# The experts' gate and up biases as three bf16 parts over 96 of 128 rows, in one pass, in place of fp32 and fp32r products over 64 rows

## The chip, the cores and the metric

The kernel runs on one core of a Trainium2 chip. The metric is the device time of one execution in microseconds (us), median of the runs shown. The engines are TensorE (PE), VectorE (DVE), ScalarE (ACT), GpSimd (POOL) and SyncE (SP), the last of which issues most DMA transfers.

## The reference, cut to what matters

Two blocks follow each other on 512 tokens of width 1024. The first (a Mamba-2 and forgetting-attention mixer and a feed-forward layer) is only touched at its end. The second has a sliding-window attention with a gated MLP, a layer norm, and 32 routed experts, of which each token takes four. All is fp32:

```python
def expert_block(args):
    xb, e = args
    gt = jnp.minimum(xb @ w_gate[e] + b_gate[e], SWIGLU_LIMIT)
    up = jnp.clip(xb @ w_up[e] + b_up[e], -SWIGLU_LIMIT, SWIGLU_LIMIT)
    hid = gt * jax.nn.sigmoid(SWIGLU_ALPHA * gt) * (up + 1.0)
    return hid @ w_down[e] + b_down[e]
```

The change concerns the two terms `b_gate[e]` and `b_up[e]`, rows of two matrices of 32 x 1024. They are added in fp32 precision.

## The kernel before, in words

Block 1 fills the first 853 us or so, the attention and gated MLP of block 2 run until about 1060 us, the router follows, and the experts run from about 1075 to 2210 us. Each instruction stands in the queue of its engine in an order that a scheduler works out from the program; the order is fixed when the kernel is built.

Matrices of weights come in fp32 from HBM. In most places one fp32 product is made of three products in fp32r, a form that goes through the array in one pass: weight and operand are split into a rounded high part (`wh`, `eh`, ...) by an ACT copy and a low part (`wl`, `el`, ...) by a DVE subtraction, and PE adds high x high, low x high and high x low into the same accumulator.

The experts are taken in the order of a rank, the fullest first for all but the first four. Even ones from the fifth on (14 of them) are small: they have 64 token rows. The other 18 are large, with 128 rows; the one at place 17 (`PS`) has two blocks of rows. Per expert there are matrices for gate (G), up (U) and down (D), each in four loads of 1 MB (`eraw`, L1061, issued on SP) into a ring of 14 slots. The order of the loads is gate and up of expert e, then down of expert e - 1.

A large expert goes through `expert_mm`: ACT casts `eh` (L1316), DVE subtracts `el` (L1317), and PE runs three fp32r products (L1382 to L1384) for each of 8 k and each half of 512 columns. A small expert goes through `expert_mm64`: PE multiplies the fp32 rows as loaded (L1398), with 64 columns of the array for one half of the outputs and the other 64 columns for the other half, so that both halves run side by side. Then DVE clamps (L1472 and L1478 are the clamps of gate and up for small experts), ACT takes the silu, and transposes (`pt_`, L1416 for the large ones) make the operands of the next products.

The bias enters as the first product of each accumulation. `bgu` holds `b_gate` in rows 0 to 63 and `b_up` in rows 64 to 127: in each, 32 rows of the rounded high part and 32 rows of the rest. The other operand picks the expert: `selP` has, in column e, a one in the row of the expert that stands at place e, repeated for each 32 rows; a column of it is broadcast over the output rows. `selr` is the same for the first four, whose place is their number. For a large expert this is a product of 64 rows in fp32r for each half (L1372); for a small one it is a product of 64 rows and 64 columns in fp32 for each half (L1391).

`bgu` is made once, at L819 to L832, when the feed-forward layer of block 1 ends: four small loads (L829) into `b0`, a tile of the ring `wraw` of three slots that also carries `w_fo`, the last matrix of block 1, and `w_in`, the first of block 2. An ACT copy makes the high part (L830), two DVE subtractions the low one (L832). Around it lies the end of the feed-forward layer: for each of 8 tiles ACT and DVE add the residual (L763, L764), subtract (L199) and sum (L206, and L207 partly on POOL), and PE makes the column sums of the norm from the last sums (L166, tile `pns`, and L171). Then the projections of block 2 start (L117 with `x2H`).

`ranks` (L1276) makes `selP` when the counts of the experts are known; `places` uses it as fp32 too. `seB` is the selection for extra blocks that are only run when an expert has more tokens than its rows hold.

Of the kernel before, what the change touches and what calls it, by code (L numbers as in the profile page):

```python
# [10 lines left out]
F32 = mybir.dt.float32  # L11
F32R = mybir.dt.float32r
# [9 lines left out]
P = 128  # L22
# [28 lines left out]
def tile_kernel(ctx, tc, I, out, dbg=None):  # L51
# [764 lines left out]
        dve.memset(tv[:, c, :, 1], float(c * P))  # L816
    dve.memset(tv[:, :, :, 2], 1.0)

    selr = pr2.tile([P, E], F32R, name="selr")  # L819
    ident4 = ident.rearrange("p (a e) -> p a e", a=4)  # L820
    selt = sb.tile([P, 2, E], F32, name="selt")
    dve.tensor_add(selt, ident4[:, :2], ident4[:, 2:])
    dve.tensor_add(selr, selt[:, 0], selt[:, 1])
    b0 = wring.tile([P, D], F32, name="b0", tag="wraw", bufs=3)
    bgu = const.tile([P, D], F32R, name="bgu", tag="csil")
    for i, nm in enumerate(("b_gate", "b_up")):
        for q in range(2):
            r = slice(64 * i + 32 * q, 64 * i + 32 * q + E)
            sp.dma_start(b0[r], I[nm])  # L829
    act.copy(bgu, b0)  # L830
    for r in (slice(32, 64), slice(96, 128)):
        dve.tensor_sub(bgu[r], b0[r], bgu[r].bitcast(F32))  # L832
    lnv = sb.tile([P, 2, 512], F32, name="lnv")
    sp.dma_start(lnv.rearrange("p a b -> p (a b)")[:, None, :], I["lnv"].partition_broadcast(P))
    wsp = sb.tile([P, 8, P], F32, name="wsp")
# [409 lines left out]
        slot_gate(ps[:, :, 3:6], n, gsl[:, sl])  # L1245

    posP = sb.tile([P, 4, E], F32, name="posP", tag="posP")
    selP = sb.tile([P, E], F32R, name="selP")
    permi = sb.tile([P, E], I32, name="permi")
    permf = sb.tile([P, 2, E], F32, name="permf")  # L1250
    rks = sb.tile([P, E], F32, name="rks")
# [24 lines left out]
    def ranks():  # L1276

        w = sm.tile([P, 4, E], F32, name="xw", tag="gt")
        key, t, kc = w[:, 0], w[:, 1], w[:, 2]
        dve.scalar_tensor_tensor(key, cnt, 64.0, iota_e, op0=OP.mult, op1=OP.subtract)  # L1280
        dve.tensor_scalar(key[:, :PRE], iota_e[:, :PRE], -1.0, 1e6, op0=OP.mult, op1=OP.add)
        for i, src in enumerate((key, cnt)):
            dve.scalar_tensor_tensor(t, src, 1.0, selr.bitcast(F32), op0=OP.mult, op1=OP.mult, accum_out=kc[:, i:i + 1])
        dve.tensor_copy(cntc, kc[:, 1:2])
        dve.tensor_scalar(t, key, kc[:, 0:1], None, op0=OP.is_gt)
        dve.tensor_reduce(kc[:, 2:3], t, axis=AX.X, op=OP.add)
        dve.tensor_scalar(selP, rks, kc[:, 2:3], None, op0=OP.is_equal)
        ps = pg.tile([2 * E, T], F32, name="ppgT", tag="pt", bufs=1)
        box["posgT"] = posgT = sm.tile([2 * E, T], F32, name="posgT", tag="up")
        for c in range(4):  # L1290
            pe.transpose(ps[:, c * P:(c + 1) * P], posg[:, c].rearrange("p a e -> p (a e)"), ident)
        act.copy(posgT, ps)

    def places():

        sf, posgT = selP.bitcast(F32), box["posgT"]
        ps = pg.tile([P, 2, 16, E], F32, name="pposP", tag="pt", bufs=1)
        for i, src in enumerate((rowe, cntc)):
            pe.matmul(ps[:, 0, 4 + i], src[:E].to_broadcast([E, P]), sf[:E], start=True, stop=True)
        for c in range(4):  # L1300
            for i in range(2):
                r = slice(i * E, (i + 1) * E)
                pe.matmul(ps[:, i, c], posgT[r, c * P:(c + 1) * P], sf[r], start=True, stop=True)
        dve.tensor_copy(permf, ps[:, 0, 4:6])
        dve.tensor_copy(permi, permf[:, 0])
        dve.tensor_copy(posP, ps[:, 0, :4])
        split_gates(PRE, E, ps[:, 1, :4])
# [58 lines left out]
    def expert_mm(xs, pss, bias=None, sel_=None, mid=None, get=ring_k):  # L1366

        if bias is not None:
            r = slice(64 * bias, 64 * bias + 64)
            for ps in pss:  # L1370
                for hf in range(2):
                    pe.matmul(ps[:, hf], sel_[r].to_broadcast([64, P]), bgu[r, hf * 512:(hf + 1) * 512],  # L1372
                              start=True, stop=False)
        for k in range(8):
            for go in (mid or {}).get(k, ()):
                go()
            for raw in get(k):
                h, l = split_k(raw)
            for (xh, xl), ps in zip(xs, pss):
                for hf in range(2):  # L1380
                    s_ = slice(hf * 512, (hf + 1) * 512)
                    pe.matmul(ps[:, hf], xh[:, k], h[:, s_], start=k == 0 and bias is None, stop=False)  # L1382
                    pe.matmul(ps[:, hf], xl[:, k], h[:, s_], start=False, stop=False)  # L1383
                    pe.matmul(ps[:, hf], xh[:, k], l[:, s_], start=False, stop=k == 7)  # L1384

    def expert_mm64(x, ps, bias=None, sel_=None, mid=None):

        for hf in range(2):
            if bias is not None:
                r = slice(64 * bias, 64 * bias + 64)  # L1390
                pe.matmul(ps[hf * 64:(hf + 1) * 64, 0], sel_[r].bitcast(F32).to_broadcast([64, 64]),  # L1391
                          bgu[r, hf * 512:(hf + 1) * 512].bitcast(F32), start=True, stop=False)
        for k in range(8):
            for go in (mid or {}).get(k, ()):
                go()
# [172 lines left out]

    ixB = sb.tile([P, 2], I32, name="ixB")
    gcB = sb.tile([P, 1], F32, name="gcB")  # L1570
    seB = sb.tile([P, 1], F32R, name="seB")

    def block(er, cl):

# [79 lines left out]
    for e in range(E):  # L1654
# [14 lines left out]
            mid[1] = [next_h(u_, "A", e - 1)]  # L1669
        if e == PS + 1:  # L1670
            mid[3] = [two_h]
        sel_ = (selr if e < PRE else selP)[:, e:e + 1]
        if small[e]:
            expert_mm64(x[0], pG[0], 0, sel_, mid)
        else:
# [213 lines left out]
```

## Time and profile before

| what | value |
|---|---|
| time, median of 3 runs | 2257.95 us (2257.52 to 2262.35) |
| the profiled execution | 2258.27 us, of which the span of the profile is 2256.5 us |
| mean granted TensorE clock | 0.973 of full speed |
| PE, DVE, ACT, POOL busy | 94%, 64%, 49%, 8% of the span |
| data moved | 554.53 MB, 246 GB/s over the span |

A group line of the profile has the source line, the engine, the operation, output <- inputs, the size of the tile of the array or of the instruction, a count and times. A matrix product in fp32 leaves two records, one in fp32r one. The products overlap in the pipeline of the array, so the time from one start to the next (the step) tells more than the duration of one record. The engines do not count waiting as busy.

### The profile page before, as it was taken

The page shows a single profiled execution, that of the slowest core. Times are in us where ns is not written, and L with a number is a line of the kernel's source. Part 1 is how long each engine was busy: PE and PEld are TensorE (multiplying, and loading weights), DVE is VectorE, ACT ScalarE, POOL GpSimd, SP SyncE. Part 2 cuts the span into 40 slices and gives each one's busy share as a digit, 9 for nine tenths or more (in the row PEclk, how much of TensorE's full clock was granted, in tenths as well). Part 3 has the DMA queues.
Part 4 walks back from the last instruction along what each step waited for, and adds up shares of the span by engine and source line. Part 5 has one row for each costly group of instructions (what it writes and reads, how often), then busy time and mean ns, then how long its engine had stood idle before and what let it go on. Part 6 is the DMA issues. An engine that isn't in the chain of part 4 may idle for free. (4 is left out here: it accounts for less than half of the span.)

```text
span 2256.5 us, 27626 instructions
## 1 busy us (share of the span) xinstructions
PE 2118.9 (94%) x9746; PEld 1495.8 (66%) x9747; DVE 1448.4 (64%) x2620; ACT 1104.4 (49%) x1511; POOL 190.4 (8%) x167
## 2 busy tenths in 40 slices
PE   7999999989999998999899999999999999899995
PEld 5787776677878886777676665445565665445653
DVE  7999978885224647655798566456553465645665
ACT  2576666434344434763576455334542455334553
POOL 0001100110000001003101110001000101001001
PEclk9999999989999998998899999999999999999998
DMA  8454414225332223136899999999997999999892
GB/s 284 139 169 145 132 61 134 94 87 174 96 100 86 94 96 97 55 123 229 291 336 347 392 401 394 405 397 349 396 358 273 367 401 396 391 365 384 337 375 81
DMA packets 153488, 554.53 MB, mean 246 GB/s; under 512 B 13440, under 2 KB 13824, under 8 KB 153344
## 3 DMA queue, kind: packets, MB, share of 16 engines
q1 hardware_dynamic: 143888, 527.54, 63.0%
q0 software_dynamic: 9456, 25.18, 4.5%
q8 instruction: 78, 1.28, 0.2%
q14 instruction: 66, 0.54, 0.1%
HBM read 537.91 MB, written 19.99 MB: 247 GB/s over the span
## 5 line engine op out<-in xcount | busy, mean ns | idle before, releaser
L1317 DVE TENSOR_TENSOR el<-eraw,eh 128x1024 fp32r<-128x1024 f32 x428 | 502.3, 1219 | 92.8 <-ACT eh L1316 81.5
L1316 ACT CAST eh<-eraw 128x1024 fp32r<-128x1024 f32 x432 | 439.5, 1048 | 137.3 <-PE ps_G L1383 49.1
L113 DVE TENSOR_TENSOR wl<-wraw,wh 128x1024 fp32r<-128x1024 f32 (+1 forms) x150 | 180.3, 1202 | 209.0 <-ACT wh L112 208.4
L112 ACT CAST wh<-wraw 128x1024 fp32r<-128x1024 f32 (+1 forms) x150 | 154.0, 1026 | 265.1 <-PE pff L118 89.8
L1384 PE MATMUL ps_G<-el,BH 128*128 128x512 f32 x288 | 114.8, 399 | 1.7 <-DVE el L1317 1.5
L1382 PE MATMUL ps_D<-eh,AH 128*128 128x512 f32 x272 | 110.7, 407 | 6.0 <-ACT eh L1316 6.0
L1382 PE MATMUL ps_G<-eh,BH 128*128 128x512 f32 x288 | 115.2, 400 | 0.0
L1384 PE MATMUL ps_D<-el,AH 128*128 128x512 f32 x272 | 111.5, 410 | 3.3 <-DVE el L1317 3.2
L1383 PE MATMUL ps_G<-eh,BL 128*128 128x512 f32 x288 | 113.3, 393 | 0.0
L1383 PE MATMUL ps_D<-eh,AL 128*128 128x512 f32 x272 | 108.9, 400 | 0.0
L1398 PE MATMUL ps_D<-eraw,AW 128*64 128x512 f32 x448 | 106.5, 603 | 0.0
L1398 PE MATMUL ps_G<-eraw,BW 128*64 128x512 f32 x448 | 103.8, 598 | 0.0
L117 PE MATMUL pff<-h2H,wh 128*128 128x512 f32 x256 | 100.7, 397 | 2.0 <-ACT h2H L733 2.0
L1384 PE MATMUL ps_U<-el,BH 128*128 128x512 f32 x256 | 102.1, 399 | 0.3 <-DVE el L1317 0.3
L117 PE MATMUL pfo<-fh,wh 128*128 128x512 f32 x256 | 100.3, 394 | 1.9 <-ACT fh L757 1.9
L118 PE MATMUL pff<-h2L,wh 128*128 128x512 f32 x256 | 101.5, 396 | 0.0
L119 PE MATMUL pff<-h2H,wl 128*128 128x512 f32 x256 | 100.3, 392 | 1.1 <-DVE wl L113 1.1
L118 PE MATMUL pfo<-fl,wh 128*128 128x512 f32 x256 | 101.4, 397 | 0.0
L1398 PE MATMUL ps_U<-eraw,BW 128*64 128x512 f32 x448 | 101.1, 604 | 0.0
L1382 PE MATMUL ps_U<-eh,BH 128*128 128x512 f32 x256 | 100.6, 393 | 0.0
L1383 PE MATMUL ps_U<-eh,BL 128*128 128x512 f32 x256 | 100.4, 392 | 0.0
L119 PE MATMUL pfo<-fh,wl 128*128 128x512 f32 x256 | 100.2, 394 | 0.0
(956 smaller groups left out, 4502.7 us busy)
## 6 DMA issues: line engine op xcount, KB each, us to landing
eraw<-in_w_gate_dram SPq DMA_DIRECT2D x128, 1024.0 KB, 10.8
eraw<-in_w_up_dram SPq DMA_DIRECT2D x127, 1024.0 KB, 11.0
eraw<-in_w_down_dram SPq DMA_DIRECT2D x127, 1024.0 KB, 10.8
wada<-in_w_ada_dram SPq DMA_DIRECT2D x48, 512.0 KB, 4.0
wraw<-in_w_fo_dram SPq DMA_DIRECT2D x32, 512.0 KB, 3.4
wraw<-in_w_ff_in_dram SPq DMA_DIRECT2D x26, 512.0 KB, 3.5
wraw<-in_w_out_dram SPq DMA_DIRECT2D x16, 512.0 KB, 3.8
wraw<-in_w_xs_dram SPq DMA_DIRECT2D x8, 512.0 KB, 6.3
```

What stands on the lines that cost most here:

```text
L112: act.copy(h, w)
L113: dve.tensor_sub(l, w, h.bitcast(F32))
L117: pe.matmul(ps, wh, xh, start=first, stop=False)
L118: pe.matmul(ps, wh, xl, start=False, stop=False)
L119: pe.matmul(ps, wl, xh, start=False, stop=last)
L1316: act.copy(h, raw_k)
L1317: (pool if ns[0] < 4 else dve).tensor_sub(l, raw_k, h.bitcast(F32))
L1382: pe.matmul(ps[:, hf], xh[:, k], h[:, s_], start=k == 0 and bias is None, stop=False)
L1383: pe.matmul(ps[:, hf], xl[:, k], h[:, s_], start=False, stop=False)
L1384: pe.matmul(ps[:, hf], xh[:, k], l[:, s_], start=False, stop=k == 7)
L1398: pe.matmul(ps[hf * 64:(hf + 1) * 64, 0], x[:, k], raw[:, hf * 512:(hf + 1) * 512], start=k == 0 and bias is None, stop=k == 7)
```

## The change

Each bias becomes three bf16 parts: the rounded value, the rounded rest and the rounded rest of that, 32 rows each, so 96 rows; rows 96 to 127 are filled with zeros by POOL. `bgu` is [128, 2, 1024] in bf16, with gate and up side by side in the columns. The selection gets bf16 copies (`selq`, `selPq`) over all 128 rows. The product of a bias is then one bf16 product over 128 rows for each half, for large (now L1382) and small experts (now L1400) alike. The set-up makes the parts on ACT (copies) and DVE (subtractions), for each bias in a `b0` tile of its own, with three loads each.

```diff
--- before.py
+++ after.py
@@ -816,20 +816,29 @@
         dve.memset(tv[:, c, :, 1], float(c * P))
     dve.memset(tv[:, :, :, 2], 1.0)
 
-    selr = pr2.tile([P, E], F32R, name="selr")
+    selr = pr2.tile([P, E], F32, name="selr")
     ident4 = ident.rearrange("p (a e) -> p a e", a=4)
     selt = sb.tile([P, 2, E], F32, name="selt")
     dve.tensor_add(selt, ident4[:, :2], ident4[:, 2:])
     dve.tensor_add(selr, selt[:, 0], selt[:, 1])
-    b0 = wring.tile([P, D], F32, name="b0", tag="wraw", bufs=3)
-    bgu = const.tile([P, D], F32R, name="bgu", tag="csil")
+    selq = pr2.tile([P, E], BF16, name="selq")
+    dve.tensor_copy(selq, selr)
+    bgu = const.tile([P, 2, D], BF16, name="bgu", tag="csil")
+    pool.memset(bgu[3 * E:], 0.0)
     for i, nm in enumerate(("b_gate", "b_up")):
-        for q in range(2):
-            r = slice(64 * i + 32 * q, 64 * i + 32 * q + E)
-            sp.dma_start(b0[r], I[nm])
-    act.copy(bgu, b0)
-    for r in (slice(32, 64), slice(96, 128)):
-        dve.tensor_sub(bgu[r], b0[r], bgu[r].bitcast(F32))
+        b0 = wring.tile([P, D], F32, name="b0", tag="wraw", bufs=3)
+        for q in range(3):
+            sp.dma_start(b0[q * E:(q + 1) * E], I[nm])
+        for q in range(3):
+            r = slice(q * E, 3 * E)
+            if q == 1:
+                for r in (slice(E, 2 * E), slice(2 * E, 3 * E)):
+                    dve.tensor_sub(b0[r], b0[r], bgu[r, i])
+                    act.copy(bgu[r, i], b0[r])
+            else:
+                if q == 2:
+                    dve.tensor_sub(b0[r], b0[r], bgu[r, i])
+                act.copy(bgu[r, i], b0[r])
     lnv = sb.tile([P, 2, 512], F32, name="lnv")
     sp.dma_start(lnv.rearrange("p a b -> p (a b)")[:, None, :], I["lnv"].partition_broadcast(P))
     wsp = sb.tile([P, 8, P], F32, name="wsp")
@@ -1245,7 +1254,8 @@
         slot_gate(ps[:, :, 3:6], n, gsl[:, sl])
 
     posP = sb.tile([P, 4, E], F32, name="posP", tag="posP")
-    selP = sb.tile([P, E], F32R, name="selP")
+    selP = sb.tile([P, E], F32, name="selP")
+    selPq = sb.tile([P, E], BF16, name="selPq")
     permi = sb.tile([P, E], I32, name="permi")
     permf = sb.tile([P, 2, E], F32, name="permf")
     rks = sb.tile([P, E], F32, name="rks")
@@ -1280,11 +1290,12 @@
         dve.scalar_tensor_tensor(key, cnt, 64.0, iota_e, op0=OP.mult, op1=OP.subtract)
         dve.tensor_scalar(key[:, :PRE], iota_e[:, :PRE], -1.0, 1e6, op0=OP.mult, op1=OP.add)
         for i, src in enumerate((key, cnt)):
-            dve.scalar_tensor_tensor(t, src, 1.0, selr.bitcast(F32), op0=OP.mult, op1=OP.mult, accum_out=kc[:, i:i + 1])
+            dve.scalar_tensor_tensor(t, src, 1.0, selr, op0=OP.mult, op1=OP.mult, accum_out=kc[:, i:i + 1])
         dve.tensor_copy(cntc, kc[:, 1:2])
         dve.tensor_scalar(t, key, kc[:, 0:1], None, op0=OP.is_gt)
         dve.tensor_reduce(kc[:, 2:3], t, axis=AX.X, op=OP.add)
-        dve.tensor_scalar(selP, rks, kc[:, 2:3], None, op0=OP.is_equal)
+        dve.tensor_scalar(selPq, rks, kc[:, 2:3], None, op0=OP.is_equal)
+        dve.tensor_copy(selP, selPq)
         ps = pg.tile([2 * E, T], F32, name="ppgT", tag="pt", bufs=1)
         box["posgT"] = posgT = sm.tile([2 * E, T], F32, name="posgT", tag="up")
         for c in range(4):
@@ -1293,7 +1304,7 @@
 
     def places():
 
-        sf, posgT = selP.bitcast(F32), box["posgT"]
+        sf, posgT = selP, box["posgT"]
         ps = pg.tile([P, 2, 16, E], F32, name="pposP", tag="pt", bufs=1)
         for i, src in enumerate((rowe, cntc)):
             pe.matmul(ps[:, 0, 4 + i], src[:E].to_broadcast([E, P]), sf[:E], start=True, stop=True)
@@ -1366,10 +1377,9 @@
     def expert_mm(xs, pss, bias=None, sel_=None, mid=None, get=ring_k):
 
         if bias is not None:
-            r = slice(64 * bias, 64 * bias + 64)
             for ps in pss:
                 for hf in range(2):
-                    pe.matmul(ps[:, hf], sel_[r].to_broadcast([64, P]), bgu[r, hf * 512:(hf + 1) * 512],
+                    pe.matmul(ps[:, hf], sel_.to_broadcast([P, P]), bgu[:, bias, hf * 512:(hf + 1) * 512],
                               start=True, stop=False)
         for k in range(8):
             for go in (mid or {}).get(k, ()):
@@ -1387,9 +1397,8 @@
 
         for hf in range(2):
             if bias is not None:
-                r = slice(64 * bias, 64 * bias + 64)
-                pe.matmul(ps[hf * 64:(hf + 1) * 64, 0], sel_[r].bitcast(F32).to_broadcast([64, 64]),
-                          bgu[r, hf * 512:(hf + 1) * 512].bitcast(F32), start=True, stop=False)
+                pe.matmul(ps[hf * 64:(hf + 1) * 64, 0], sel_.to_broadcast([P, 64]),
+                          bgu[:, bias, hf * 512:(hf + 1) * 512], start=True, stop=False)
         for k in range(8):
             for go in (mid or {}).get(k, ()):
                 go()
@@ -1568,7 +1577,7 @@
 
     ixB = sb.tile([P, 2], I32, name="ixB")
     gcB = sb.tile([P, 1], F32, name="gcB")
-    seB = sb.tile([P, 1], F32R, name="seB")
+    seB = sb.tile([P, 1], BF16, name="seB")
 
     def block(er, cl):
 
@@ -1669,7 +1678,7 @@
             mid[1] = [next_h(u_, "A", e - 1)]
         if e == PS + 1:
             mid[3] = [two_h]
-        sel_ = (selr if e < PRE else selP)[:, e:e + 1]
+        sel_ = (selq if e < PRE else selPq)[:, e:e + 1]
         if small[e]:
             expert_mm64(x[0], pG[0], 0, sel_, mid)
         else:
```

The scheduler orders the rest anew. On PE, at the down products of one small expert (`ps_D`, L1398 before, L1407 now), the two halves of the up bias of the next small expert (L1391 before, L1400 now) stand as follows; `pt_` are transposes. Before:

```order
L1398 MATMUL ps_D<-eraw,AW 64x512 x4
L1391 MATMUL ps_U<-bgu,selP 64x512
L1398 MATMUL ps_D<-eraw,AW 64x512 x4
L1416 MATMUL pt__15412<-ident,up 128x128 x5
L1398 MATMUL ps_D<-eraw,AW 64x512 x4
L1416 MATMUL pt__15412<-ident,up 128x128 x3
L1391 MATMUL ps_U<-bgu,selP 64x512
L1398 MATMUL ps_D<-eraw,AW 64x512 x4
```

And now:

```order
L1407 MATMUL ps_D<-eraw,AW 64x512 x4
L1400 LDWEIGHTS selPq
L1400 MATMUL ps_U<-bgu,selPq 64x512
L1407 MATMUL ps_D<-eraw,AW 64x512 x4
L1425 MATMUL pt__13486<-ident,up 128x128 x8
L1400 LDWEIGHTS selPq
L1400 MATMUL ps_U<-bgu,selPq 64x512
L1407 MATMUL ps_D<-eraw,AW 64x512 x8
```

The halves are apart in both; the transposes stand together now, and the load of the selection is an instruction of its own.

On DVE, where block 1 ends, a piece of the difference: `t` and `nS` are the residual and the sums of the feed-forward layer's end, `wl` a split of `w_in`, `b_7386` and `b_7397` the `b0` tiles of the gate and the up bias. The lines of the change (L836, L840) are the subtractions of the parts.

```order
-L832 TENSOR_TENSOR bgu<-b_7382,bgu 32x1024
-L113 TENSOR_TENSOR wl<-wraw,wh 128x1024
-L832 TENSOR_TENSOR bgu<-b_7382,bgu 32x1024
+L836 TENSOR_TENSOR b_7386<-b_7386,bgu 32x1024 x2
+L113 TENSOR_TENSOR wl<-wraw,wh 128x1024
+L840 TENSOR_TENSOR b_7386<-b_7386,bgu 32x1024
 L764 SCALAR_TENSOR_TENSOR t_3850<-pfo,modp,xa_7248 128x512
+L836 TENSOR_TENSOR b_7397<-b_7397,bgu 32x1024
 L199 TENSOR_TENSOR t_3850<-t_3850,nm_6023 128x512
+L764 SCALAR_TENSOR_TENSOR t_3850<-pfo,modp,xa_7268 128x512
 L206 TENSOR_TENSOR nS<-nS,t_3850 128x512
```

Three subtractions stand ahead of the first L764 where two stood; of the other three, one is shown behind that L764, and two more follow it ahead of the last L206. A `wl` of 128x768 moves from before the last L199 to behind the last L207.

## Rows read from the trace of the kernel before

**Rows 1.** The page's list of engines: busy us, share of the span, instructions.

```profile
PE 2118.9 (94%) x9746; PEld 1495.8 (66%) x9747; DVE 1448.4 (64%) x2620; ACT 1104.4 (49%) x1511; POOL 190.4 (8%) x167
```

**Rows 2.** Table by stretches, core 0: columns as in the head row.

```profile
core 0: us, PE busy (x) PEld busy (x) DVE busy (x) ACT busy (x) POOL busy (x), PEclk, DMA share, GB/s
867.00:1060.00 193.00, 184.71 (x964) 149.18 (x964) 115.01 (x282) 111.81 (x202) 13.32 (x19) 0.97 0.36 124
1240.00:1680.00 440.00, 419.45 (x1909) 249.66 (x1906) 257.55 (x413) 198.75 (x208) 39.07 (x27) 0.99 1.02 390
1680.00:1720.00 40.00, 40.00 (x177) 28.79 (x177) 18.00 (x15) 10.87 (x11) 0.97 (x1) 1.00 0.53 183
```

**Rows 3.** Waits of SP's DMA queue: waited for: us in total, times, longest.

```profile
SPq L1061 <- DVE el L1317: 463.8, 173, 24.2
```

**Rows 4.** Who waited for the loads of L1061 (us, times).

```profile
  PEld ps_U L1398: 3.8, 11
```

**Rows 5.** Waits of PE, 1240 to 2210 us.

```profile
PE ps_G L1372 <- DVE gt L1472: 11.9, 10, 4.8
```

**Rows 6.** Groups by line, PE, 1070 to 2210 us: busy us, mean ns.

```profile
L1391 PE MATMUL ps_U<-bgu,selP 64*64 64x512 f32 x56 | 25.7, 614 | 0.0
```

**Rows 7.** Timeline of PE: a pair of small gate-bias halves (start, us).

```profile
1841.69 0.39 PE L1382 MATMUL ps_U<-eh,BH 128*128 128x512 f32 x1
1841.92 0.39 PE L1383 MATMUL ps_U<-eh,BL 128*128 128x512 f32 x1
1842.24 1.07 PE L1391 MATMUL ps_G<-bgu,selP 64*64 64x512 f32 x4
1843.24 0.51 PE L1384 MATMUL ps_U<-el,BH 128*128 128x512 f32 x1
```

**Rows 8.** Timeline of PE: one small up-bias half alone.

```profile
1854.49 1.07 PE L1391 MATMUL ps_U<-bgu,selP 64*64 64x512 f32 x2
1855.48 1.51 PE L1398 MATMUL ps_D<-eraw,AW 128*64 128x512 f32 x6
```

**Rows 9.** Timeline of PE: a small matrix, and a large one's first product.

```profile
1874.12 7.09 PE L1398 MATMUL ps_U<-eraw,BW 128*64 128x512 f32 x32
...
1883.33 0.50 PE L1382 MATMUL ps_D<-eh,AH 128*128 128x512 f32 x1 [0.60 <-ACT eh L1316]
```

**Rows 10.** Timeline of PE: a pair of large bias products inside a stream.

```profile
1828.16 0.72 PE L1372 MATMUL ps_U<-bgu,selP 64*128 64x512 f32 x2
1828.81 0.50 PE L1384 MATMUL ps_G<-el,BH 128*128 128x512 f32 x1
```

**Rows 11.** Timeline of DVE where block 1 ends.

```profile
844.16 1.22 DVE L832 TENSOR_TENSOR bgu<-b,bgu 32x1024 fp32r<-32x1024 f32 x1
845.95 0.75 DVE L764 SCALAR_TENSOR_TENSOR t<-pfo,modp,xa 128x512 f32<-128x512 f32 x1 [0.56 <-PE pfo L119]
...
855.03 1.36 DVE L113 TENSOR_TENSOR wl<-wraw,wh 128x768 fp32r<-128x768 f32 x1
...
857.02 0.69 DVE L206 TENSOR_TENSOR nS<-nS,t 128x512 f32<-128x512 f32 x1
```

**Rows 12.** Timeline of ACT, the same stretch.

```profile
839.83 1.05 ACT L830 CAST bgu<-b 128x1024 fp32r<-128x1024 f32 x1
...
846.73 0.63 ACT L763 ACTIVATE xa<-t 128x512 f32<-128x512 f32 x1 [3.86 <-DVE t L764]
...
851.49 0.84 ACT L112 CAST wh<-wraw 128x768 fp32r<-128x768 f32 x1 [0.61 <-PE pfo L118]
```

**Rows 13.** Timeline of PE: the column sums of the norm.

```profile
857.77 1.87 PE L166 MATMUL pns<-ones,nS 128*128 128x1 f32 x8 [4.77 <-DVE nS L206]
```

**Rows 14.** The page's DMA issues: KB each, us to landing.

```profile
wraw<-in_w_fo_dram SPq DMA_DIRECT2D x32, 512.0 KB, 3.4
```

**Rows 15.** Last up matrix: its loads' issue and landing, and its casts.

```profile
2157.17 8.73 SPq L1061 DMA_DIRECT2D eraw<-in_w_up_dram  x4
...
DMA to landing us min/median/max: 11.5/12.1/14.7
...
2182.41 3.89 ACT L1316 CAST eh<-eraw 128x1024 fp32r<-128x1024 f32 x4
```

## The prediction

> **What bounds the kernel now.** I read the list of engines first: PE is busy for 2118.9 us, 94% of the span, and the next engine, DVE, for 1448 us [rows 1]. An average does not say what one stage is worth, so the table by stretches comes second. In the expert phase from 1240 to 1680 us PE is busy for 419.45 of 440 us at a granted clock of 0.99, DVE for 258 and ACT for 199; the DMA share there is 1.02, so two resources look full at once [rows 2]. Which of the two ends last is read from the waits. Weight loads are issued on SP at L1061, and SP's longest wait there is for a free ring slot, which DVE's subtraction L1317 gives back: 463.8 us over 173 waits [rows 3]. In the other direction hardly anybody waits for a weight that has not landed: the fp32 products of the U matrices do so 11 times for 3.8 us in all [rows 4]. In the stretch 1680 to 1720 us the DMA share falls to 0.53 while PE is busy for 40.00 of 40 us [rows 2]. So the loads wait for PE's side, and PE is the bound. What PE idles there is hand-offs, the most of it ten waits for DVE's clamp of the gate (L1472, 11.9 us in all), each ahead of a bias product of a large expert [rows 5]. PE time taken out of its busy stream shortens the run; time taken out just ahead of a wait does not.
>
> **Part 1: the bias products of the small experts (L1391).** 14 small experts x (G, U) x 2 column halves make 56 products; the grouped view has 56 records for the U products, and as many for G, which is two records for each fp32 product [rows 6]. Where the halves stand next to each other they run side by side: the pair at 1842.24 takes four records and the next product starts 1843.24 - 1842.24 = 1.00 us later [rows 7]. Where the planner left them apart, one half alone takes the same: from 1854.49 to 1855.48, 0.99 us [rows 8]. Reading all of them in the timeline I count 17 pairs (one is shown) and 22 halves alone (one is shown), 39 places of 1.00 us on PE, together 39.0 us. The first listing of the order shows such halves apart, and that they stay apart. What does such a place consist of? A whole fp32 matrix of a small expert (8 k, halves side by side) takes the 7.09 us that begin at 1874.12, which is 0.886 for each k [rows 9]; fp32 goes through four times, so 0.222 for one pass of 512 columns. Rows of fp32r agree: steps of 0.23 us [rows 7]. The place has 1.00 - 0.886 = 0.11 on top, paid on the way from and to the neighbouring products. The new product is one bf16 pass over 128 rows and 64 columns, so I take 0.222 + 0.11 = 0.33 us; the trace of before has no bf16 product of this shape. The nearest row is the fp32r bias product of large experts, which takes (1828.81 - 1828.16) / 2 = 0.33 us each [rows 10]. Saved: 39 x (1.00 - 0.33) = 26.1 us. Bounds: with nothing on top, 0.22 for each place, 39 x 0.78 = 30.4; if the load of its own selection weights is not hidden and the halves no longer overlap, half the place goes, 39 x 0.50 = 19.5.
>
> The Trainium skill ("TensorEngine Tiling (Array Packing)", Tiling Modes, Key Properties) says that changing the tiling mode drains the engine. The trace agrees: the step into the 64-row product at 1842.24 is 0.32 us, that between its ordinary neighbours 0.23 [rows 7]. By that rule the 22 halves alone, which stand among 128-row, 64-column products, would drop the 0.11 too, as they no longer change the mode; part 1 would be 2.4 us more and the time 2225.
>
> **Part 2: the bias products of the large experts (L1372).** 18 large experts, one of them with two blocks, make 38 pairs of products. A pair inside a stream takes 0.65 us, 1828.16 to 1828.81 [rows 10]. Two ordinary 128-row products step 2 x 0.23 = 0.46 us [rows 7]. So a pair in a stream saves 0.2 in itself, and about 0.2 at its two edges, as 64-row products have a step of 0.32 into them instead of 0.23 [rows 7]: of the 38 about 16 stand so, 16 x 0.4 = 6.4 us. Ten G pairs begin after the wait for the gate's clamp [rows 5]; they save their own 0.17: 1.7 us. Ten U pairs are followed by a wait of 0.60 us for the ACT cast of a down matrix [rows 9], which would only get longer: nothing. Two stand at the start-up, nothing. Sum 8.1 us; bounds 3 (no gain at the edges) and 10.
>
> **Part 3: the set-up, once, at 840 to 867 us.** Before: one ACT copy of 1.05 us and two subtractions of 1.22 us on 32 rows [rows 11, 12]. After: eight ACT copies and six such subtractions, in the order that the listing of DVE's order shows. Cover on ACT: it idles 3.86 us at one place there [rows 12]. DVE has less: it is late behind PE by only 0.56 us at 845.95 and then runs without a gap to the last column-sum operand at 857.02 [rows 11], and PE waits 4.77 us for just that operand (L206) before the sums of the norm [rows 13]. So what enters DVE's order between the first L764 and the last L206 comes out at PE: three subtractions, 3 x 1.22 = 3.7 us. A weight split of 1.36 us [rows 11] moves out behind them, into the time in which PE makes the sums. The first L764 is queued behind the last subtraction of the gate's bias, which itself waits for a copy on ACT: +0.3. Together about +2.7 us. Two small copies of 32 columns (`selq` before the second block's projections, `selP` behind the ranks) stand on the chain: 0.1 each. Sum +2.9. Hidden are the POOL fill (POOL is busy for 8% of the span [rows 1]) and the copies on ACT. On SP the loads of the biases go from four to six, and the second bias takes a slot of its own in the three-slot ring, so the first load of `w_in` behind it has to wait for one more slot of the last `w_fo` tiles, to about 845. The cast L112 that reads it ran at 851.49 [rows 12], and 512 KB land in 3.4 us [rows 14]: no stall. From 867 to 1060 us PE is busy 184.71 of 193 us [rows 2], so nothing swallows the delay. Bounds: +1.5 (only the chain's own lateness) and, if copies and subtractions of both biases run strictly one behind the other, 2 x (3 x 1.05 + 3 x 1.22) = 13.6 against 1.05 + 2 x 1.22 = 3.5 before: +10.1.
>
> **What is late next.** With PE some 34 us faster over the expert phase, loads must be issued earlier; they can, because their slots come free earlier, as long as the queue has room. At the end the margin shows: the four loads of the last up matrix are issued from 2157.17, land 11.5 to 14.7 us later, so the first about 2169, and the cast of the same matrix ran in the burst that begins at 2182.41 [rows 15], its third of four at 2182.41 + 2 x 0.97 = 2184.4: 15 us of margin. In between the queue has idle room of some 20 us (1680 to 1720 at 0.53) to catch up in [rows 2]. So I cost the loads at nothing.
>
> **The sum.** -26.1 - 8.1 + 2.9 = -31.3 us, on the profiled execution's 2258.27 us (span 2256.5 and 1.8 outside it): 2227 us. The median of the runs shown is 2257.95, 0.3 below the profiled one, so nothing has to be shifted. 0.2% is 4.5 us, about what a measurement of this kernel can tell from no change.
>
> **Rivals.**
> The loads become the bound. For it: DMA share 1.02 over 440 us [rows 2]. If no load of the last experts could come earlier, the gain would end with the 15 us of margin: 2258 - 15 = 2243. Against it: SP waits for slots, not slots for SP [rows 3, 4], and the share of 0.53 later. Chance 0.11.
> The bf16 places are dearer: selection loads are not hidden, halves apart do not overlap. 19.5 + 3 - 2.9 = 19.6 saved: 2239. For it: the trace has no such product. Against: fp32 products of the same 64 columns run at 0.222 a pass with their loads hidden [rows 9]. Chance 0.12.
> The edges go everywhere, since a full-height product no longer changes anything in the array for its neighbours: 30.4 + 10 - 2.9 = 37.5: 2221. For it: the pairs and the halves alone both pay an edge today [rows 7, 8]. Against: a 64-column product still stands in a 128-column stream at the 17 pairs. Chance 0.12.
> The change doesn't shorten a place at all, since issue and load and not the passes fill it: then only the set-up is left, 2258 + 2.9 = 2261, no change. Against: four passes fill 0.886 of 1.00 us. Chance 0.04.
> Slower: the split of both biases runs serially over the hand-offs between ACT and DVE, each L763 on ACT and L764 on DVE queued behind a split step, and +10.1 us reach PE, which waits for L206. It decides only where the products give back under 10.1 - 4.5 = 5.6 us, that is at places above 0.87 us; with places that gave nothing: 2268. For it: PE's 4.77 us wait for DVE is there [rows 13]. Against: 0.87 us for one pass is far from 0.33. Chance 0.03 for a run that is slower by over 0.2%. With places at 0.33 the same serial split gives 2234, inside the range.
> The forecast itself, 2218 to 2236, has 0.58.
>
> **How the numbers follow.** Predicted 2227. The range goes from 2215 (all edges and the cheap set-up, 30.4 + 10 - 1.5 = 38.9, make 2219; 4 more for the measurement) to 2245 (dear places with the serial set-up, 19.5 + 3 - 10.1 = 12.4, make 2246; the capped loads 2243). Faster by over 0.2%: 0.58 + 0.11 + 0.12 + 0.12 = 0.93, from which I take 0.02 for a reordering of the small experts' work by the planner that costs what the products gain: 0.91. Within 0.2%: 0.05. Slower: 0.04.
>
> **What would show it.** Right: the fp32 group of 64 x 64 is gone and its successor's places step 0.3 to 0.36 us; pairs of the large experts step 0.46; PE's wait for the clamp L1472 stays about 12 us; the wait of the norm's sums for L206 grows from 4.77 to about 7.5; the stretch from the first to the last expert loses some 34 us, the one before it gains about 3. Wrong: waits of the eh casts or of the fp32 products for loads of tens of us (loads), places of 0.5 us and more (dear slots), a start of the projections later than 868 by 8 us or more (serial split).

## The result, and the profile after

| | before | after |
|---|---|---|
| median of the runs | 2258.70 us (4 runs, 2257.52 to 2262.35) | 2228.65 us (4 runs, 2226.82 to 2229.13) |
| ratio, 95% interval | | 0.9863 (0.9851 to 0.9875) |
| profiled execution, its span | 2258.27, 2256.5 us | 2229.12, 2227.5 us |

The forecast was 2227 us, a gain of 31.3; measured is 30.0. PE is still what bounds the kernel. The list of engines after, which answers to [rows 1], and the stretches that answer to [rows 2] (columns as there):

```profile
PE 2077.3 (93%) x9690; PEld 1499.3 (67%) x9691; DVE 1452.0 (65%) x2626; ACT 1109.6 (50%) x1518; POOL 193.4 (9%) x168
...
872.00:1065.00 193.00, 183.13 (x971) 146.77 (x972) 114.97 (x282) 111.71 (x202) 12.48 (x19) 0.98 0.34 123
1240.00:1669.00 429.00, 404.83 (x1883) 252.74 (x1880) 256.55 (x414) 197.16 (x208) 36.65 (x27) 0.99 1.03 396
1669.00:1707.00 38.00, 38.00 (x172) 27.95 (x172) 17.46 (x15) 10.88 (x11) 0.97 (x1) 1.00 0.63 226
```

PE's busy time fell by 2118.9 - 2077.3 = 41.6 us and the span by 29.0, so 12.6 us of it came back as time in which PE isn't busy. The DMA share in the full stretch went from 1.02 to 1.03 and the loads kept up: those who wait for a load do so for little, as before [rows 4].

```profile
  PEld ps_D L1407: 2.8, 9
  PEld ps_G L1407: 2.6, 10
  PEld ps_U L1407: 2.3, 6
```

Where the span went is read from two landmarks on PE's timeline, the first projection of block 2 and the first product of the closing sum (`ps_pt`). The kernel before, then after:

```profile
867.65 1.65 PE L117 MATMUL pi<-x2H,wh 128*128 128x512 f32 x3 [3.14 <-ACT x2H L852]
2207.31 0.49 PE L1764 MATMUL ps_pt<-lent,gT 96*128 96x512 f32 x1 [0.50 <-DVE BL L1418]
```

```profile
872.59 1.65 PE L117 MATMUL pi<-x2H,wh 128*128 128x512 f32 x3 [3.23 <-ACT x2H L861]
2176.84 0.50 PE L1773 MATMUL ps_pt<-lent,gT 96*128 96x512 f32 x1 [0.51 <-DVE BL L1427]
```

The first comes 4.9 us later, the second 30.5 earlier: between them 35.4 us are gained. Of the last 1.5 us that are lost again, the granted clock tells the cause. In the last down product it fell to half for some 3 us (0.53 in the row, the lower of its two levels, 1.2 GHz, for most of the stretch), after PE had been busy for 3.4 of 6 us (2176 to 2182 us); in the same place before it stood at 1.00 (2213 to 2216 us). Over all 14 profiles of this case the time from that landmark to the end is 50.6 to 51.0 us in the eight where the clock falls in that product, and 49.2 to 49.5 us in the six where it doesn't.

```profile
2182.50:2185.50 3.00, 3.00 (x8) 2.32 (x8) 3.00 (x4) 2.26 (x3) 0.00 (x0) 0.53 0.53 77
```

The new products by group, on PE from 1070 us on. They answer to [rows 6]:

```profile
L1400 PE MATMUL ps_U<-bgu,selPq 128*64 128x512 bf16 x28 | 9.4, 391 | 0.0
L1382 PE MATMUL ps_G<-bgu,selPq 128*128 128x512 bf16 x30 | 9.1, 378 | 10.5 <-DVE gt L1481 9.5 <-ACT yo L1505 1.1
L1400 PE MATMUL ps_G<-bgu,selPq 128*64 128x512 bf16 x28 | 6.0, 398 | 0.0
```

One record for each product instead of two, and the wait for the clamp is there still: 9.5 us in ten times, 11.9 before [rows 5].

A pair of small gate halves in a large expert's stream, PE's timeline, as in [rows 7]:

```profile
1825.42 0.40 PE L1392 MATMUL ps_U<-eh,BH 128*128 128x512 f32 x1
1825.65 0.39 PE L1393 MATMUL ps_U<-eh,BL 128*128 128x512 f32 x1
1825.97 0.41 PE L1400 MATMUL ps_G<-bgu,selPq 128*64 128x512 bf16 x2
1826.63 0.50 PE L1394 MATMUL ps_U<-el,BH 128*128 128x512 f32 x1 [0.25 <-DVE el L1328]
```

The place is 1826.63 - 1825.97 = 0.66 us, not 0.33, and 0.25 of it is a wait for `el` that the longer fp32 pair had hidden. The step into it is 0.32 still. And the up halves that stand apart, as in [rows 8]:

```profile
1836.16 1.94 PE L1407 MATMUL ps_D<-eraw,AW 128*64 128x512 f32 x8
1837.93 0.38 PE L1400 MATMUL ps_U<-bgu,selPq 128*64 128x512 bf16 x1
1837.93 2.09 PE L1407 MATMUL ps_D<-eraw,AW 128*64 128x512 f32 x8
1839.95 1.09 PE L1425 MATMUL pt__14993<-ident,up 128*128 128x128 f32 x8
1840.98 0.40 PE L1400 MATMUL ps_U<-bgu,selPq 128*64 128x512 bf16 x1
1840.98 3.83 PE L1407 MATMUL ps_D<-eraw,AW 128*64 128x512 f32 x16
1844.46 2.06 PE L1407 MATMUL ps_G<-eraw,BW 128*64 128x512 f32 x8
```

Here the bias half and the next weight product start at the same time, 1837.93: one takes one half of the array's columns, the other the other half. From the first down product to the first gate product are 1844.46 - 1836.16 = 8.30 us.

The set-up: PE's wait for the last operand of the column sums, which answers to [rows 13].

```profile
862.63 1.87 PE L166 MATMUL pns<-ones,nS 128*128 128x1 f32 x8 [7.92 <-DVE nS L206]
```

7.92 instead of 4.77: 3.15 us more. On DVE the first residual step and that last operand are 861.89 - 847.56 = 14.3 us apart, where they were 11.1 [rows 11], with three of the new subtractions between them:

```profile
847.56 0.75 DVE L764 SCALAR_TENSOR_TENSOR t<-pfo,modp,xa 128x512 f32<-128x512 f32 x1
861.89 0.68 DVE L206 TENSOR_TENSOR nS<-nS,t 128x512 f32<-128x512 f32 x1
```

The remaining 4.9 - 3.15 = 1.8 us of the first landmark had built up ahead of that wait, most of it in block 1, which is the same in both kernels; in the profiles of this case PE comes to that wait at 852.7 to 859.4 us.

### The profile page after: what moved, and what is told of

It is laid out like the page before. It is cut to its first block, busy times and chain, and to the rows that moved or that the text cites. A ratio compares the mean times of both kernels' runs of the same rounds, so it can differ in the third digit from the quotient of the medians.

```text
span 2227.5 us, 27531 instructions
## 1 busy us (share of the span) xinstructions
PE 2077.3 (93%) x9690; PEld 1499.3 (67%) x9691; DVE 1452.0 (65%) x2626; ACT 1109.6 (50%) x1518; POOL 193.4 (9%) x168
## 5 line engine op out<-in xcount | busy, mean ns | idle before, releaser
L1394 PE MATMUL ps_G<-el,BH 128*128 128x512 f32 x288 | 116.3, 404 | 1.7 <-DVE el L1328 1.5
L1394 PE MATMUL ps_D<-el,AH 128*128 128x512 f32 x272 | 109.2, 401 | 5.1 <-DVE el L1328 5.1
L1407 PE MATMUL ps_G<-eraw,BW 128*64 128x512 f32 x448 | 110.1, 619 | 0.0
L1394 PE MATMUL ps_U<-el,BH 128*128 128x512 f32 x256 | 102.9, 402 | 3.4 <-DVE el L1328 3.3
L1407 PE MATMUL ps_D<-eraw,AW 128*64 128x512 f32 x448 | 106.0, 597 | 0.0
L1407 PE MATMUL ps_U<-eraw,BW 128*64 128x512 f32 x448 | 101.5, 603 | 0.0
```

The costliest lines, as they stand in the source:

```text
L1407: pe.matmul(ps[hf * 64:(hf + 1) * 64, 0], x[:, k], raw[:, hf * 512:(hf + 1) * 512], start=k == 0 and bias is None, stop=k == 7)
```

## The experiments

Ratios are to the kernel before in the same set of runs, with 95% intervals; a thousandth is 2.26 us. e1 to e4 share a set, and so do e5 to e8, e9 with e10, and e11 with e12; the last two sets ran on other chips.

| run | what | median us | ratio (95%) |
|---|---|---|---|
| e1 | before, set-up early | 2258.09 | 0.9998 (0.9989 to 1.0007) |
| e2 | large experts' products new | 2253.30 | 0.9973 (0.9964 to 0.9982) |
| e11 | e2 again | 2253.33 | 0.9965 (0.9951 to 0.9979) |
| e9 | large: fp32r, 128 rows | 2257.95 | 0.9996 (0.9987 to 1.0005) |
| e12 | e9, masks on POOL | 2256.16 | 0.9973 (0.9964 to 0.9983) |
| e5 | the changed kernel again | 2228.67 | 0.9861 (0.9843 to 0.9878) |
| e3 | changed, set-up early | 2225.70 | 0.9844 (0.9831 to 0.9858) |
| e4 | e3, small bias behind the 4th k | 2224.52 | 0.9846 (0.9833 to 0.9860) |
| e8 | e4, halves apart | 2227.23 | 0.9849 (0.9829 to 0.9869) |
| e6 | e3 without small biases | 2225.18 | 0.9847 (0.9830 to 0.9865) |
| e7 | e3, large: bf16 over 64 rows | 2230.36 | 0.9868 (0.9851 to 0.9886) |
| e10 | e7, up pair twice | 2230.43 | 0.9872 (0.9857 to 0.9887) |

**e1, the old set-up out of the way.**

```diff
+            if f == 18:               # in the feed-forward layer of block 1
+                bias_parts_old()      # the old loads, copy and subtractions
-    b0 = wring.tile(...)              # ... at their old place
```

> The kernel before, with its own set-up of the biases (one copy, two subtractions) moved to the middle of the feed-forward layer of block 1, where DVE is busy less than half of the time. Products as before. Theory: in the kernel before the set-up is nearly hidden, since DVE is late behind PE by only 0.56 us at its first residual step; the time stays within 2.5 us of before (2256 to 2259). Rival: the two subtractions of 1.22 us are on the path in full and 2.4 us or more go, 2256 or less, with PE's wait for the last column-sum operand falling from 4.77 to about 2.3 us.

Measured 0.9998; PE's wait for the last operand 4.07 us instead of 4.77. The old set-up cost some 0.7 us at that wait, and the ratio, good to 2 us, shows no more; theory.

**e2 and e11, the large experts alone.**

```diff
 # in expert_mm64 only: the fp32 product of before, on the new tile read as fp32
+                r = slice(64 * bias, 64 * bias + 64)
+                pe.matmul(..., sel_[r].bitcast(F32).to_broadcast([64, 64]), bgo[r, ...].bitcast(F32), ...)
```

> The new parts and the new bf16 products for the large experts; the small experts keep the fp32 products of 64 rows and 64 columns (they read the new tile as fp32, so the values of the small experts' biases are meaningless here, the instructions are those of before). Both sets of parts are made early, in the feed-forward layer, so nothing of the set-up is in the difference to e1. Theory (part 2 of the forecast): 8 us less than e1, between 3 and 10, all of it from pairs inside a stream. Rival: the large pairs give nothing, since they stand at waits; then within 1.5 us of e1.

> e2 once more (large experts' products in bf16 over 128 rows, small ones as before, set-up early), beside e12 with the same runs of before, since e2 and e9 differed by 5 us where their places on PE are alike. Theory: the height of the product is what counts, and the difference between e2 and e9 was the four masks on DVE ahead of the second block's first operand (about 1.2 us) and the spread between sets of runs; then e11 and e12 lie within 2 us of each other, 3 to 6 us below before. Rival: bf16 gives something that the places don't show; then e11 again 5 us below e12.

e2 is 0.0025 below e1, 5.6 us; e11 0.0033, 7.5 us, each good to 3 or 4 us. The part is real and inside its bounds, somewhat under the 8 that were forecast. The pair in a stream came out as reckoned. After (start to start 0.23 into the pair, 0.26 for the pair, 0.42 for the product behind it):

```profile
1129.47 0.39 PE L1394 MATMUL ps_G<-el,BH 128*128 128x512 f32 x1
1129.70 0.61 PE L1382 MATMUL ps_U<-bgu,selq 128*128 128x512 bf16 x2
1129.96 0.58 PE L1392 MATMUL ps_U<-eh,BH 128*128 128x512 f32 x1
1130.38 0.39 PE L1393 MATMUL ps_U<-eh,BL 128*128 128x512 f32 x1
```

From 1129.47 to 1130.38 are 0.91 us, and four ordinary steps of 0.23 would be 0.92, so the pair costs its two passes and nothing else. Before, the pair alone took 0.65 with 0.1 at each edge [rows 10, 7].

**e3 and e5, the new set-up out of the way.**

```diff
+            if f in (18, 24):         # in the feed-forward layer of block 1
+                bias_parts(*((0, "b_gate") if f == 18 else (1, "b_up")))
-    for i, nm in enumerate(("b_gate", "b_up")):    # ... at its place behind the layer
```

> The changed kernel, with the set-up of the parts moved to the middle of the feed-forward layer; all else as changed. Theory (part 3): the set-up costs about 3 to 4 us on the path at the end of the feed-forward layer; PE's wait for the last column-sum operand falls from 7.92 us to 4 or less and the time by 3 to 5 us against the changed kernel, to about 2224. Rival: the serial split is hidden and what block 1 lost in the one profile (1.2 us ahead of the set-up, half a clock step at the end) is chance; then 2227 to 2229. Against e2 the theory expects 26 us less (part 1), the rival for dear places 19.5.

> The changed kernel itself, once more, beside kernels that share e3's early set-up, so that the set-up's price is read with one set of runs of before. Theory: the new set-up costs 7.92 - 4.08 = 3.8 us at the last column-sum operand (PE's wait for L206 in the two profiles); ratio to before 3 to 5 us above e3's 0.9844, about 0.986. Rival: what the profile of e3 shows in the feed-forward layer (+6 us against before ahead of the set-up) is the price of the early place and not chance; then the two are equal within 1.5 us.

e3 is 0.9844, the changed kernel 0.9863 and 0.9861: 3.8 to 4.3 us, with intervals that overlap. The mechanism is sharper in the profile, PE's same wait in e3:

```profile
863.30 1.87 PE L166 MATMUL pns<-ones,nS 128*128 128x1 f32 x8 [4.08 <-DVE nS L206]
```

7.92 - 4.08 = 3.8 us, what the medians say. The first projection itself starts no earlier in e3's profile (873.27, after 872.59 us), since PE came to the wait 4.5 us later; that lies within the spread from 852.7 to 859.4, so a price of the early place of a microsecond or two is neither shown nor excluded. Against e2 and e11, e3 prices part 1 alone: 0.9973 - 0.9844 = 0.0129, 29 us, and by e11 0.0121, 27 us, each good to 4 us. e3 has the lowest ratio of all, and the set-up needn't be paid where it was.

**e4, the small bias moved among the small products.**

```diff
-        for hf in range(2):           # ahead of k = 0, start=True
+            if k == 3 and bias is not None:
+                for hf in range(2):
+                    pe.matmul(ps[hf * 64:(hf + 1) * 64, 0], sel_.to_broadcast([P, 64]),
+                              bgu[:, bias, hf * 512:(hf + 1) * 512], start=False, stop=False)
```

> As e3, and the two bias products of a small expert's matrix come after the products of its fourth k, side by side, in place of ahead of them. They then stand among 128-row products of 64 columns, not in the stream of a large expert. In the profile of the changed kernel 11 gate pairs inside a large expert's stream take 0.655 us, 0.25 of it a wait for the el subtraction, and have edges of 0.1 us on both sides; among the small products a pair takes 0.22. Theory of the edges: 11 x (0.655 + 0.2 - 0.22) = 7 us less than e3. Rival: the wait for el is only moved to the next product of the large expert; 11 x 0.4 = 4 us less. Second rival: the halves that stand alone in the changed kernel cost nothing there, and 0.22 for each of ten pairs is paid back: 2 us less for each of the two figures.

Equal to e3, and all the numbers of the expectation missed (the trace has ten such pairs, not eleven). With the pair gone from the large stream, PE waits longer there for the same subtraction, 5.9 us in ten times instead of 2.5. In e4:

```profile
1825.02 0.39 PE L1398 MATMUL ps_U<-eh,BL 128*128 128x512 f32 x1
1825.99 0.50 PE L1399 MATMUL ps_U<-el,BH 128*128 128x512 f32 x1 [0.58 <-DVE el L1333]
```

From the one product to the other are 0.97 us without the pair, and 1826.63 - 1825.65 = 0.98 with it in the changed kernel. So the move gains nothing there, and among the small products a pair takes 0.22, ten of them 2.2 us, too little to be seen. On DVE's timeline (after) the reason is the large gate's clamp L1469, which goes ahead of the subtraction that PE is due to use:

```profile
1824.22 1.23 DVE L1469 TENSOR_SCALAR gt<-ps_G 128x1024 f32<-128x1024 f32 x1 [1.51 <-PE ps_G L1394]
1825.36 3.48 DVE L1328 TENSOR_TENSOR el<-eraw,eh 128x1024 fp32r<-128x1024 f32 x3
```

The first of the three subtractions of 1.2 us ends near 1826.6, and L1394 starts at 1826.63. So a pair of 0.4 us that stands there is free.

**e6, no small bias products at all.**

```diff
-            expert_mm64(x[0], pG[0], 0, sel_, mid)
+            expert_mm64(x[0], pG[0], None, None, mid)
-            expert_mm64(x[0], pU[0], 1, sel_)
+            expert_mm64(x[0], pU[0])
```

> As e3, without the bias products of the small experts (their gate and up biases are left out). It prices what these products still cost. Theory from the traces after: a matrix whose two halves stand apart pays one pass, 0.22 us, since each half runs beside the other half's product of L1407; a gate pair inside a large stream covers a wait for el and costs next to nothing. 10 x 0.22 for the U matrices apart, some 6 pairs at 0.22, the rest covered: 3 to 5 us less than e3. Rival (the forecast's place): 39 places x 0.33 = 13 us less.

0.9847 against e3's 0.9844: no saving that the medians can show. The forecast's 13 us are far outside; the 3 to 5 of the theory were not seen either, though they are within the intervals' reach, and the runs of e6 had the lower mean granted clock, 0.9744 against 0.9756. Its profile has the wait for `el` at 5.9 us in ten, as e4. The stretch of down products at the same expert takes 1841.73 - 1833.64 = 8.09 us, against 8.30 with the two halves apart in the changed kernel, so 0.21 for both, one pass:

```profile
1833.64 3.65 PE L1412 MATMUL ps_D<-eraw,AW 128*64 128x512 f32 x16
1837.23 1.09 PE L1430 MATMUL pt__14955<-ident,up 128*128 128x128 f32 x8
1838.25 3.65 PE L1412 MATMUL ps_D<-eraw,AW 128*64 128x512 f32 x16
1841.73 1.89 PE L1412 MATMUL ps_G<-eraw,BW 128*64 128x512 f32 x8
```

**e8, the halves apart on purpose.**

```diff
-            if k == 3 and bias is not None:
-                for hf in range(2):
+            for hf in range(2):
+                if bias is not None and k == (2, 5)[hf]:
```

> As e4, but the two halves of each small bias stand apart on purpose, one behind the third k and one behind the sixth. Theory: apart costs what together costs, 0.22 for each matrix, since the half that is ahead runs beside the other half's fp32 product until the second half evens it out: equal to e4 within 1.5 us. Rival: each half apart costs a place of its own (as the fp32 halves of before did): 28 x 0.22 = 6 us more than e4.

0.9849 against 0.9846; theory, but the intervals together reach 5 us, and the rival's 6 lie at their edge. The rows decide: a U matrix with the pair behind it, e4 first and e8 second.

```profile
1991.10 3.65 PE L1410 MATMUL ps_U<-eraw,BW 128*64 128x512 f32 x16
1999.19 0.59 PE L1387 MATMUL ps_U<-bgu,selPq 128*128 128x512 bf16 x2 [0.79 <-DVE up L1494]
```

```profile
1997.08 2.79 PE L1408 MATMUL ps_U<-eraw,BW 128*64 128x512 f32 x12
2005.17 0.59 PE L1387 MATMUL ps_U<-bgu,selPq 128*128 128x512 bf16 x2 [0.79 <-DVE up L1492]
```

Both take 8.09 us, and without the bias products (e6) it is 7.88. So two halves of 64 columns over 128 rows cost one pass, 0.21 us, together or apart, as long as they stand among others of that shape; the one half that stands ahead of a product of 128 columns (after, 1208.04 us) took 0.33.

**e7, bf16 over 64 rows.**

```diff
-                    pe.matmul(ps[:, hf], sel_.to_broadcast([P, P]), bgu[:, bias, ...], ...)
+                    pe.matmul(ps[:, hf], sel_[:64].to_broadcast([64, P]), bgu[:64, bias, ...], ...)
```

> As e3, but the large experts' bias product is bf16 over rows 0 to 63 alone (two of the three parts; the third is left out). It separates the height of the product from its type. Theory of the edges: the 64-row form pays the edges again; a pair in a stream goes from 0.255 + 0.42 for itself and the next step back to about 0.65 + 0.34, 14 to 16 pairs x 0.4 = 6 us more than e3, and steps of the granted clock to one half between the G, U and D products of the later large experts come back. Rival: the type alone made the difference; then equal to e3 within 1.5 us and no more such steps.

0.9868, 5.4 us above e3, good to 5 us. PE's timeline at the place that is shown under e2:

```profile
1124.63 0.40 PE L1399 MATMUL ps_G<-el,BH 128*128 128x512 f32 x1
1124.95 0.60 PE L1387 MATMUL ps_U<-bgu,selq 64*128 64x512 bf16 x2
1125.49 0.50 PE L1397 MATMUL ps_U<-eh,BH 128*128 128x512 f32 x1
1125.82 0.39 PE L1398 MATMUL ps_U<-eh,BL 128*128 128x512 f32 x1
```

1.19 us from first to last start instead of 0.91: the edges of 0.32 and 0.33 are back although the type is bf16.

**e9 and e12, fp32r over 128 rows.**

```diff
+            if isinstance(sel_, list):      # per bias, zero in the other bias's 64 rows
+                sel_, r, m = sel_[bias], slice(0, P), P
-                    pe.matmul(ps[:, hf], sel_[r].to_broadcast([64, P]), bgu[r, ...], ...)
+                    pe.matmul(ps[:, hf], sel_[r].to_broadcast([m, P]), bgu[r, ...], ...)
```

> As e1 (old parts in fp32r, small experts as before), but the large experts' bias product goes over all 128 rows in fp32r, with a selection that is zero in the other bias's 64 rows. It is the other half of e7: the height without the type. Theory: the height is what the large part gained; as e2, 5 to 6 us less than e1 (ratio about 0.997), a pair in a stream at about 0.25 to 0.45 us plus a next step of 0.42 at most, and no step of the granted clock at the hand-offs of the last large experts (before: 1958, 2095, 2163 us). Rival: bf16 was what mattered; then as e1, within 1.5 us.

> As e9 (fp32r over 128 rows, the other bias's rows masked by zeros in the selection), with the masks made on POOL, off the path. Theory: 1 to 1.5 us less than e9 and within 2 us of e11, ratio to before 0.997 to 0.9985. Rival: as e9, 0.9995 or more, and 5 us above e11.

e9 showed nothing, 0.9996, though its places on PE are those of e12. In it DVE made the masks with six small instructions right ahead of the first projection's operand; from the column sums to that projection are 10.8 us in e9 and 8.9 in e12, 1.9 of the 5 us between their ratios. The rest stays unexplained: the two medians lie 1.8 us apart, those of before in the two sets 1.9 (2259.14 and 2260.99 us). With the masks on POOL the ratio is 0.9973, within 2 us of e11. The old fp32r form over all rows, e12's timeline:

```profile
1126.09 0.40 PE L1407 MATMUL ps_G<-el,BH 128*128 128x512 f32 x1
1126.33 0.63 PE L1395 MATMUL ps_U<-bgo,selr 128*128 128x512 f32 x2
1126.79 0.39 PE L1405 MATMUL ps_U<-eh,BH 128*128 128x512 f32 x1
1127.02 0.39 PE L1406 MATMUL ps_U<-eh,BL 128*128 128x512 f32 x1
```

0.93 us in place of 0.91: for a pair in a stream the height did it, not bf16. The drain between tiling modes that the Trainium skill states ("TensorEngine Tiling (Array Packing)", Tiling Modes, Key Properties) agrees with e7 and e12 together. Over the 16 pairs that stand in a stream, places and edges are 6.2 us shorter than before in e2 and in the changed kernel and 5.3 in e12, and e7 gives 4.3 back. Behind the clamp it is the type: a G pair there takes 0.65 us before and 0.66 in e12, but 0.52 in e7 and in the changed kernel, 1.3 us for ten.

**e10, the up pair twice.**

```diff
-            for ps in pss:
-                for hf in range(2):
+            for ps, hf, l_ in [(p_, h_, q_) for p_ in pss
+                               for q_ in range(bias * (len(pss) == 1), -1, -1) for h_ in range(2)]:
...
-                              start=True, stop=False)
+                              start=True, stop=l_ == 1)
```

> As e7 (bf16 over 64 rows for the large experts), but the up bias of a large expert with one block is issued twice, the second product overwriting the first; result as e7's. The extra pair, 0.53 us, stands ahead of PE's wait of 0.74 us for the eh cast of the down product, so it should cost no time of its own. Theory: the steps of the granted clock at these hand-offs follow PE's idle time and its half-height products there together; filling most of the wait removes the steps that e7 has at 1439, 1508, 1866, 2006 and 2071 us, 1.5 us each, so 3 to 7 us less than e7 although PE does more. Rival: filling with half-height products doesn't count; the steps stay, and the time is e7's or up to 2 us more.

Equal to e7, 0.9872: the 3 to 7 us of the theory are not seen. The extra pair is hidden at nine hand-offs, where the place takes 1.32 us with one pair and with two, but in five streams it adds 0.43 us each, 2.2 in all, which the expectation left out. Of the five steps that the expectation names, four are gone from e10's profile; the same stretch of e7 and of e10 (granted clock 0.89 and 1.00):

```profile
2000.00:2015.00 15.00, 13.00 (x51) 8.75 (x48) 11.89 (x12) 10.04 (x10) 0.00 (x0) 0.89 1.02 412
```

```profile
2000.00:2015.00 15.00, 13.43 (x61) 9.38 (x58) 13.38 (x13) 11.07 (x11) 0.00 (x0) 1.00 1.02 413
```

The other runs say so too: the mean granted clock is 0.974 over e7's four and 0.977 over e10's. What that is worth stays open: the two ratios together are good to 5 us, so the medians neither show nor exclude what is left of the gain.

## Why the prediction was right

**The bound** was right. PE stays full, loads are in time, and the gain is PE's.

**Part 1** (26.1 forecast) measured 27 to 29 us, within its bounds, but its uniform place of 0.33 us was wrong both ways, and that the sum came out near is luck. The 22 halves alone were mis-sized: 20 of them belong to ten U matrices, and two of them cost 0.21 us together, since each runs beside a weight product of the other half of the columns. The stretch that takes 8.30 us now took 1863.16 - 1852.62 = 10.54 before:

```profile
1852.62 1.94 PE L1398 MATMUL ps_D<-eraw,AW 128*64 128x512 f32 x8
1863.16 1.89 PE L1398 MATMUL ps_G<-eraw,BW 128*64 128x512 f32 x8
```

So such a stretch gained 2.24 us, 1.79 of them (2 x 1.00 - 0.21) at the halves, where 2 x 0.67 = 1.34 was forecast; the rest came at the edges and from the transposes, which stand together now. The fp32 halves of before, over 64 rows, took 1.00 us each and shared nothing; whether the height or the type lets the new ones share a pass, no run separates. The pairs in a large stream gave less: from the product ahead to the product behind are 1843.24 - 1841.92 = 1.32 us before [rows 7] and 0.98 now, a gain of 0.34 and not 0.67, because the wait for `el` takes up the rest. Only nine of the 17 pairs stood in such a stream, not all 17, as the rival on the edges has it. The step that takes 0.222 + 0.11 = 0.33 us for every place put one price on both cases; the excess of one and the lack of the other nearly cancelled. The rule that the prediction weighed there (the Trainium skill, "TensorEngine Tiling (Array Packing)", Key Properties) pointed the right way for the halves alone, but the 2.4 us drawn from it were too few.

**Part 2** (8.1 forecast) measured 5.6 and 7.5 us, and by the rows 6.2 + 1.3 = 7.5. The reckoning at the edges holds by row: 0.41 us for a pair in a stream. A G pair behind the clamp gave 0.13 instead of 0.17; a U pair nothing, as forecast: the wait behind it grew from 0.60 to 0.73 us. The mean granted clock of the runs rose too, from 0.9735 in e1 to 0.9765 in e2; the forecast had no such term, and its share of the gain is not separated.

**Part 3** (+2.9 forecast) measured 3.15 us at the named wait, and 3.8 to 4.3 us against a set-up out of the way, where the old one by the same measure cost 0.5 to 0.7. The order of DVE said it: three subtractions in PE's way. No load of `w_in` was late.

**The rivals.** Loads as the bound: no. Dear places: true only of the pairs in a stream. Everything at the edges (2221): in kind for the halves alone. Serial split, slower: the split did reach PE, for 3 us and not 10 (and the place at which it would have decided is 1.00 - 5.6 / 39 = 0.86 us, not 0.87).

## What to carry to other kernels

Price a product by where it stands, not by its passes alone: a product whose tile of the array differs from its neighbours' pays at both edges, and two of half the columns, one for each half, among others of that shape pay one pass between them. Before shortening something on the bound engine, look at what its neighbour waits for behind it: time that covered a wait turns into the wait. A one-time set-up belongs where its engines idle: early, the medians here were 3.8 to 4.3 us lower.

## What the runs showed that was not expected

Two halves of 64 columns over 128 rows cost one pass of 0.21 us even 3 us apart (8.30 against 8.09 us for the stretch). The rows of e6 say 3 to 4 us and its median shows none, while untouched code of block 1 moved by up to 7 us between profiles, and the mean granted clock of the runs moved with the kernel (e7, e10): at this size a stage of the trace and a median of several runs have to agree before either is believed.
